# Five dummy products out, input blocks issued behind the first weight half, and the last weight sums moved behind group 0's weighing, in a two-layer decoder trunk

## The chip, the cores and the metric

The kernel runs on one core of one Trainium2 chip. The metric is the device time of one execution in microseconds; a time is the median of the runs shown.

## The reference

The reference computes two decoder layers over a residual stream h of 512 positions by 1024 features, all in float32. Only the first layer's start matters here:

```python
def dilated_mixer(xn, w_qkv, w_o, cos, sin):
    qkv = xn @ w_qkv                          # 12 heads of 64
    q, k, v = jnp.split(qkv, 3, axis=-1)
    ...                                       # rotary on q and k
    for g, (window, r) in enumerate(A_GROUPS):    # (128,1), (512,4), (2048,16): 4 heads each
        ...                                   # banded attention on every r-th position
        outs.append(o)
        lses.append(lse)
    alpha = jax.nn.softmax(jnp.stack(lses, axis=0), axis=0)
    o = jnp.concatenate([outs[g] * alpha[g][..., None].astype(outs[g].dtype)
                         for g in range(len(A_GROUPS))], axis=2)
    return o.reshape(B, T, A_WIDTH) @ w_o

def reference(...):
    h = x
    for l in range(DEPTH):                    # l = 0: dilated_mixer, l = 1: forgetting attention
        ...
        h = h + rms_norm(mix, g[1])
        f = conv_ffn(rms_norm(h, g[2]), w_up[l], conv_w[l], conv_b[l], w_down[l])
        h = h + rms_norm(f, g[3])
    return h
```

So three groups of heads are attended to separately, their outputs are weighed by a softmax over the groups ("weighing"), joined, and projected by w_o. Then follows a gated feed-forward network with a causal convolution of width 3.

## The kernel before

The 512 positions are four blocks of 128 on the partitions (`h[:, b, :]`). Every float32 product is made as three matmuls of a high part and a low part (high by high, high by low, low by high); the high part is a rounded copy made by ACT (ScalarE), the low part the rest, made by DVE (VectorE). TensorE (PE) sums them in eight PSUM banks of 128x512. All instructions of an engine run in the order in which the program wrote them; there is no scheduler that moves them. Waits between engines are by semaphores, which are put in from the tiles that each instruction reads and writes.

Nearly all loads go through one queue, SP's, in program order. Its semaphores are eight, taken in turn, so that an issue also waits for the landing of the one eight places before it. `Weights.load(n)` issues the loads up to weight piece n; `Weights.high` and `low` make the two parts of a piece, `get` hands out the next one and makes parts ahead (`W.ahead`).

**The start.** SP loads x in 256 KB pieces, block by block: `load_x(i, *blocks)` loads feature half i of these blocks. The first weight piece is loaded in two halves (`early[0][:, 0]`). `warm_up(n)` writes n dummy products of a zero tile into a bank that nobody reads; these come ahead of the first transposes. `gcol0` holds the norm gains of layer 0 as columns, which are multiplied into the weights. The lines:

```python
    W.load(1)
    load_x(0, 1, 2, 3)
    ...
    warm_up(4)
    ...                                    # transpose of the gain row, copy to gcol0
    warm_up(5)
    ...
    pool.tensor_copy(early[0][:, 1, 0:1], early[0][:, 0, 0:1])
    W.load(2)
    load_x(1, 0, 1)
```

The copy on POOL (GpSimd) reads the first weight half and writes one element a partition of the tile that the second piece is loaded into. So SP's load of the second piece stands until the first half has landed. After that block 0's first four feature chunks are transposed (`transposed0`, L1283), with two more dummies behind (`warm_up(2)`). ACT makes the high part (`high0`, L1287), DVE the low part (`low0`, L1291); `first_weight(k)` and `first_low(k)` (L1303, L1305, L1309) do so for the two halves of the first weight. `one0(b, kc, n)` is one of the three products of block b and feature chunk kc (L1320), and `split0(i, *blocks)` transposes and splits further blocks. Then q and k of group 0 follow for all blocks and chunks (`qk0`).

**The weight sums.** The down projection of the feed-forward networks is done with fewer products from sums of blocks of w_down. `down_sums` is a generator that makes these sums a step at a time: a step issues the loads of one pair of row blocks (L588 to L590), makes the four DVE sums (L593 to L596) of the pair one step before, and stores the pair one step before that to a buffer in device memory (`dT`, L601, two DMAs of 512 KB from SP). The generator `down0` has twelve pairs: (0,0) to (0,10) for layer 0 and (1,8) for layer 1, so 14 steps. Two steps are taken in `v_proj0`, and one behind each of the four weight pieces of three calls of `wide_proj` (q and k of group 1, q and k of group 2, v of groups 1 and 2). In the last of these the third step makes the sums of (1,8) and stores (0,10), and the fourth stores (1,8).

**From attention to the feed-forward network.** Behind the last `wide_proj`, written out by hand: `pv(g, pr)` multiplies probabilities and values (L1220, L1223), `weigh(g, pr)` transposes the group's factors on PE (L1239) and multiplies on DVE (L1241), `p_transpose` copies transposed probabilities on ACT (L1169), and `combine(g, pr)` makes the high and low part of the weighed output (L1251 on ACT, L1252 on DVE). Then SP loads the convolution's rows (L565, L566), two gain rows, two gains (L231), the last two pieces of w_o and the first of w_up (L50). The output projection (`Proj.finish`) does two of six chunks for blocks 0 and 1, then a hook transposes the convolution rows on PE (L573), copied by DVE (L575), then the two chunks for blocks 2 and 3, then the other four chunks. Before its first result is squared by ACT (L332), ACT makes the high parts of the next w_up pieces (L60) and DVE the low parts (L78), in program order. Of each block the projection's result is normed, added to h, normed again (`xn`, L311) and transposed (L361); the transposes of block 0 stand on PE between the projection's products.

Of the kernel before, what the change touches and what calls it, by code (L numbers as in the profile page):

```python
# [117 lines left out]
def trunk_kernel(ctx, tc, x, norm_gains, w_qkv_a, w_o_a, w_q_b, w_o_b, kv_norm, w_kvf, b_f,  # L118
                 w_up, conv_w, conv_b, w_down, rope, out):
    nc = tc.nc  # L120
    act, dve, pool, pe, sp = nc.scalar, nc.vector, nc.gpsimd, nc.tensor, nc.sync
# [8 lines left out]
    def t8(shape, dt=F32, name="t8"):  # L130
        return p8.tile(shape, dt, tag="t8", name=name)

    def t4(shape, dt=F32, name="t4"):
        return p4.tile(shape, dt, tag="t4", name=name)

    def t2(shape, dt=F32, name="t2"):
        return p2.tile(shape, dt, tag="t2", name=name)

    def bank(shape, name="bank"):
        return psp.tile(shape, F32, tag="ps", name=name)  # L140
# [16 lines left out]
    for g in range(3):  # L157
        for s in range(4):
            def f(raw, g=g, s=s):
                v = raw.rearrange("p (k t c) -> p k t c", k=2, t=2)  # L160
                src = wqkv.rearrange("(k p) (t c) -> p k t c", p=128, c=256)
                return [(v[:, k], src[:, 2 * s + k, g:g + 4:3, :]) for k in range(2)]
# [45 lines left out]
    early = []  # L208
# [13 lines left out]
    h = cst.tile([128, NB, D], F32, name="h")  # L222

    def load_x(i, *blocks):
        s = slice(i * 512, (i + 1) * 512)
        for b in blocks:
            sp.dma_start(h[:, b, s], xv[b * 128:(b + 1) * 128, s])
# [12 lines left out]
    zero = t2([128, 512], BF16, name="zero")  # L240
    dve.memset(zero, 0.0)
    warm = bank([128, 512], name="warm")

    def warm_up(n, c=512):
        for i in range(n):
            pe.matmul(warm[:, :c], zero[:, 0:128], zero[:, :c], start=True, stop=True)
    W.load(1)
    load_x(0, 1, 2, 3)
    rp = t4([128, 8, 32], name="rope")
    act.activation(sml.tile([128, 1], F32, tag="sd", name="warm"), eps_t, AF.Sqrt)  # L250

# [5 lines left out]
    pe.transpose(pg0, g_row, ident[:8, :8])  # L257
    gcol0 = sml.tile([128, 8], F32, tag="gcol0", name="gcol0", bufs=1)
    dve.tensor_copy(gcol0, pg0)
    warm_up(5)  # L260

    def columns(*ks):
        return [gcol0[:, k:k + 1] for k in ks]
# [14 lines left out]
    same = cst.tile([128, 4], F32, name="same")  # L278


    pool.tensor_copy(early[0][:, 1, 0:1], early[0][:, 0, 0:1])
    W.load(2)
    load_x(1, 0, 1)
    W.load(3)
# [4 lines left out]
    def mm3(o, ah, al, bh, bl, first, last, shared=False):  # L289
        pe.matmul(o, ah, bh, start=first, stop=False, skip_group_check=shared)  # L290
        pe.matmul(o, ah, bl, start=False, stop=False, skip_group_check=shared)  # L291
        pe.matmul(o, al, bh, start=False, stop=last, skip_group_check=shared)  # L292
# [285 lines left out]
    def down_sums(pairs, place, queue, lag, behind):  # L578


        live, n = [], len(pairs)
        for i in range(n + lag + behind):
            if i < n:
                l, j = pairs[i]
                a, b = place()
                live.append((a, b))
                r = w_down[l][j * 256:j * 256 + 256, :].rearrange("(c p) d -> c p d", p=128)
                sp.dma_start(a, r[0])  # L588
                sp.dma_start(b[:, 0:512], r[1, :, 512:1024])
                sp.dma_start(b[:, 512:1024], r[1, :, 0:512])  # L590
            if 0 <= i - lag < n:
                a, b = live[i - lag]
                dve.tensor_tensor(a[:, 0:512], a[:, 512:1024], a[:, 0:512], ALU.subtract)  # L593
                dve.tensor_tensor(a[:, 512:1024], b[:, 0:512], a[:, 512:1024], ALU.subtract)
                dve.tensor_tensor(b[:, 0:512], b[:, 0:512], a[:, 0:512], ALU.subtract)
                dve.tensor_tensor(b[:, 512:1024], b[:, 512:1024], b[:, 0:512], ALU.subtract)  # L596
            i -= lag + behind
            if i >= 0:
                l, j = pairs[i]
                for q, t in enumerate(live[i]):  # L600
                    queue.dma_start(dT[l][j, :, q * 1024:q * 1024 + 1024], t)  # L601
            yield
# [489 lines left out]
    def ax(g, b, kc):  # L1092
        return xs(xP if g else xT, kc, slice(b * 128, b * 128 + 128))
# [116 lines left out]
    def pv(g, pr):  # L1210
        o = bank([128, T], name="o_ps")
        for b in range(4):
            for hh in range(2):
                hd = 2 * pr + hh
                ov = o[64 * hh:64 * hh + 64, b * 128:(b + 1) * 128]
                vs = slice(hd * 64, hd * 64 + 64)
                if g == 0:
                    ks = [0, 1] if b else [1]
                    for k in ks:
                        pe.matmul(ov, V[g][:, b - 1 + k, vs], PT[g][hh][:, b, 2 * pr + k, :],  # L1220
                                  start=k == ks[0], stop=k == 1)
                else:
                    pe.matmul(ov, V[g][:, b, vs], PT[g][0][:, b, 2 * hh + pr, :], start=True, stop=True)  # L1223
        if g == 2:
            ow[g, pr] = o
            return
        ow[g, pr] = t = t2([128, T], name="ow")
        if g == 0:
            act.copy(t, o)
        else:  # L1230
            act.copy(t.rearrange("p (l r) -> p r l", r=4), o.rearrange("p (r l) -> p r l", r=4))
# [3 lines left out]
    def weigh(g, pr):  # L1235

        fb = bank([128, 4, 128], name="f_ps")
        for r in range(4):
            pe.transpose(fb[:, r, :], fac[g][:, r, 2 * pr:2 * pr + 2, :].rearrange("p h d -> p (h d)"), ident)  # L1239
        t = ow[g, pr].rearrange("p (l r) -> p r l", r=4)  # L1240
        dve.tensor_tensor(t, t, fb, ALU.mult)  # L1241

    def combine(g, pr):
        t = ow.pop((g, pr))
        if pr == 0:
            OT[g] = t8([128, 2, 2, T], F32R, name=f"OT{g}")
        hi, lo = (OT[g][:, part, pr, :] for part in range(2))
        if g == 2:
            t = t.rearrange("p (r l) -> p r l", r=4)
            hi, lo = (a.rearrange("p (l r) -> p r l", r=4) for a in (hi, lo))  # L1250
        act.copy(hi, t)  # L1251
        dve.tensor_tensor(lo, t, hi.bitcast(F32), ALU.subtract)  # L1252
# [27 lines left out]
    def transposed0(b, i):  # L1280
        pt = bank([128, 4, 128], name="xt_ps")
        for k in range(4):
            pe.transpose(pt[:, k, :], h[:, b, (4 * i + k) * 128:(4 * i + k + 1) * 128], ident)  # L1283
        return pt

    def high0(b, i, pt):
        act.copy(xT[0][i][:, :, b * 128:b * 128 + 128], pt)  # L1287

    def low0(b, i, pt):
        s = slice(b * 128, b * 128 + 128)  # L1290
        dve.tensor_tensor(xT[1][i][:, :, s], pt, xT[0][i][:, :, s].bitcast(F32), ALU.subtract)  # L1291

    def split0(i, *blocks):
        pts = [transposed0(b, i) for b in blocks]
        for b, pt in zip(blocks, pts):
            high0(b, i, pt)
            low0(b, i, pt)
# [9 lines left out]
    def first_low(k):  # L1307
        s, g = slice(512 * k, 512 * k + 512), columns(k)[0]
        dve.scalar_tensor_tensor(w0[:, 1, s], raw0[:, s], g, w0[:, 0, s].bitcast(F32), ALU.mult, ALU.subtract)  # L1309

    def weight0(s):
        if s not in ws:
            ws[s] = [t.rearrange("p (k c) -> p k c", k=2) for t in W.get()]
        return ws[s]

    def one0(b, kc, n):
        if b not in qk_banks:
            qk_banks[b] = bank([128, T], name="qk_ps")
        w, a = weight0(kc // 2), ax(0, b, kc)
        pe.matmul(qk_banks[b], a[n == 2], w[n == 1][:, kc % 2, :], start=kc + n == 0, stop=kc + n == KD + 1)  # L1320
# [13 lines left out]
    first_low(0)  # L1334
    first_weight(1)
    one0(0, 0, 0)
    warm_up(1, 128)
    one0(0, 0, 1)
    low0(0, 0, pt)
    one0(0, 1, 0)  # L1340
    first_low(1)
    one0(0, 0, 2)
    split0(0, 1)
    one0(0, 1, 1)
    one0(0, 1, 2)
# [42 lines left out]
    reorder(act.copy, 2, 3, parts=(0,))  # L1388
    sums = down_sums([(1, 6), (1, 7)], in_two, sp, 1, 3)
    next(sums)  # L1390
    def wide_proj(g, name, post, between):

        banks = [bank([128, T], name=name) for _ in range(4)]
        for s in range(4):
            w = W.get()
            wh, wl = (t.rearrange("p (k c) -> p k c", k=2) for t in w)
            for b in range(4):
                for k in range(2):
                    kc = 2 * s + k
                    ah, al = ax(g, b, kc)  # L1400
                    mm3(banks[b], ah, al, wh[:, k, :], wl[:, k, :], kc == 0, kc == KD - 1)
                if s == 3:
                    post(g, b, banks[b])
            for f in between[s]:
                f()
            next(down0, None)

    def v_post(g, b, o):
        if b == 0:
# [5 lines left out]
    down0 = down_sums([*[(0, j) for j in range(ND)], (1, 8)], in_one, sp, 1, 1)  # L1415
# [14 lines left out]
        [L(p_transpose, 1, 2), L(p_transpose, 1, 3), L(qk_transpose, 2, 0), L(qk_transpose, 2, 1)],  # L1430
        [L(qk_transpose, 2, 2), L(qk_transpose, 2, 3), L(scores, 2, 0, 1)],
        [L(scores, 2, 2, 3), factors],
        []])
    pv(0, 0)
    pv(0, 1)
    weigh(0, 0)
# [4 lines left out]
    pv(1, 0)  # L1441
    pv(1, 1)
    combine(0, 1)
    weigh(1, 0)
    weigh(1, 1)
    combine(1, 0)
# [420 lines left out]
```

## Time and profile before

| | us |
|---|---|
| runs | 1103.29, 1100.98, 1102.45 |
| median | 1102.45 |
| the profiled execution | 1101.57 |
| its span, from the first to the last instruction | 1099.8 |
| PE busy | 1092.0 (99%) |
| DVE busy | 877.4 (80%) |
| ACT busy | 671.1 (61%) |
| POOL busy | 174.4 (16%) |

The profile is of one execution. A row of the timeline reads: start in us from the span's start, duration in us, engine, source line, operation, what it writes from what it reads, shape, count; in brackets how long the engine stood idle before it and what ended that. PEld is PE's weight load, which overlaps PE. A "q" behind an engine is its sequencer: SPq rows are the issue of DMAs, not their transfer. Rows of equal operations are merged, and the duration is then that of all of them. A matmul's end is modelled, so that a stream of products is read by the distance of its starts.

### The profile page before, as it was taken

The page shows a single profiled execution, that of the slowest core. Times are in us where ns is not written, and L with a number is a line of the kernel's source. Part 1 is how long each engine was busy: PE and PEld are TensorE (multiplying, and loading weights), DVE is VectorE, ACT ScalarE, POOL GpSimd, SP SyncE. Part 2 cuts the span into 40 slices and gives each one's busy share as a digit, 9 for nine tenths or more (in the row PEclk, how much of TensorE's full clock was granted, in tenths as well). Part 3 has the DMA queues.
Part 4 walks back from the last instruction along what each step waited for, and adds up shares of the span by engine and source line. Part 5 has one row for each costly group of instructions (what it writes and reads, how often), then busy time and mean ns, then how long its engine had stood idle before and what let it go on. Part 6 is the DMA issues. An engine that isn't in the chain of part 4 may idle for free.

```text
span 1099.8 us, 18080 instructions
## 1 busy us (share of the span) xinstructions
PE 1092.0 (99%) x6600; PEld 951.0 (86%) x6600; DVE 877.4 (80%) x1496; ACT 671.1 (61%) x1116; POOL 174.4 (16%) x246
## 2 busy tenths in 40 slices
PE   9999999999999999999999999999999999999997
PEld 6988889899999988888878888889899999988886
DVE  4897888888778689897687667858888788679994
ACT  6755575755656747576452587755756666647572
POOL 3633001311111211000000212101311111211000
PEclk9999999999999999999999999999999999999999
DMA  9699764467987979894446767784468878989872
GB/s 319 198 343 409 304 200 134 102 176 190 211 194 184 249 252 331 291 324 117 134 154 223 266 192 199 243 246 135 91 179 190 211 185 188 240 267 320 308 249 77
DMA packets 192130, 242.67 MB, mean 221 GB/s; under 512 B 12848, under 2 KB 138792, under 8 KB 192040
## 3 DMA queue, kind: packets, MB, share of 16 engines
q1 hardware_dynamic: 176408, 189.33, 53.2%
q0 software_dynamic: 14944, 52.18, 20.6%
q8 instruction: 52, 0.85, 0.3%
q14 instruction: 38, 0.31, 0.1%
q10 hardware_dynamic: 688, 0.01, 0.0%
HBM read 172.37 MB, written 39.73 MB: 193 GB/s over the span
## 4 chain that ended last, share of the span: by engine, by line
PE 99%; DVE 1%; issue 0%; ACT 0%; DVEq 0%; ACTq 0%
PE up L291 13%; PE up L290 13%; PE up L292 13%; PE acc L290 9%; PE acc L292 9%; PE acc L291 9%; PE v_ps L290 2%; PE v_ps L292 2%; PE v_ps L291 2%; PE qk_ps L1320 2%; PE pT_ps L1708 2%; PE o_ps L1723 2%; PE s_ps L1674 2%; PE qk_ps L290 1%; PE first L292 1%; PE first L290 1%
## 5 line engine op out<-in xcount | busy, mean ns | idle before, releaser
L290 PE MATMUL acc<-w 128*128 128x512 f32 (+1 forms) x311 | 120.6, 388 | 0.3 <-DVE mix L339 0.3
L292 PE MATMUL acc<-w 128*128 128x512 f32 (+1 forms) x311 | 120.4, 387 | 0.0
L291 PE MATMUL acc<-w 128*128 128x512 f32 (+1 forms) x267 | 103.2, 387 | 0.0
L290 PE MATMUL up<-xsh,w 128*128 128x256 f32 x352 | 99.6, 283 | 0.0
L291 PE MATMUL up<-xsl,w 128*128 128x256 f32 x352 | 99.6, 283 | 0.0
L292 PE MATMUL up<-xsh,w 128*128 128x256 f32 x352 | 99.6, 283 | 0.0
L78 DVE TENSOR_TENSOR w<-wraw,w 128x1024 fp32r<-128x1024 f32 x62 | 82.3, 1342 | 21.2 <-ACT w L60 19.2
L627 ACT ACTIVATE bb<-up,conv 128x512 f32<-128x512 f32 x80 | 59.5, 775 | 58.8 <-DVE up L1014 48.0
L60 ACT CAST w<-wraw 128x1024 fp32r<-128x1024 f32 x81 | 83.6, 1050 | 19.0 <-DMA wraw<-in_w_up_dram 8.2
L291 PE MATMUL up<-xbl,w 128*128 128x512 f32 (+1 forms) x276 | 93.5, 339 | 0.0
L291 PE MATMUL up<-xcl,w 128*128 128x512 f32 (+1 forms) x276 | 93.5, 339 | 0.0
L290 PE MATMUL up<-xbh,w 128*128 128x512 f32 (+1 forms) x276 | 93.5, 339 | 0.0
L290 PE MATMUL up<-xch,w 128*128 128x512 f32 (+1 forms) x276 | 93.5, 339 | 0.0
L292 PE MATMUL up<-xbh,w 128*128 128x512 f32 (+1 forms) x276 | 93.4, 338 | 0.0
L292 PE MATMUL up<-xch,w 128*128 128x512 f32 (+1 forms) x276 | 93.4, 338 | 0.0
L290 PEld LDWEIGHTS acc<-w 128*128 128x128 f32 x311 | 58.4, 188 | 12.4 <-DVE mix L339 0.7
L292 PEld LDWEIGHTS acc<-w 128*128 128x128 f32 x311 | 58.4, 188 | 12.0
L290 PEld LDWEIGHTS up<-xsh,w 128*128 128x128 f32 x352 | 67.6, 192 | 0.0
L291 PEld LDWEIGHTS up<-xsl,w 128*128 128x128 f32 x352 | 67.6, 192 | 0.0
L292 PEld LDWEIGHTS up<-xsh,w 128*128 128x128 f32 x352 | 67.6, 192 | 0.0
L628 DVE SCALAR_TENSOR_TENSOR bb<-up,conv,bb 128x511 f32<-128x511 f32 x80 | 59.5, 744 | 6.4 <-ACT bb L627 6.2
L630 DVE SCALAR_TENSOR_TENSOR bb<-up,conv,bb 128x510 f32<-128x510 f32 x80 | 59.9, 749 | 2.8
(316 smaller groups left out, 3104.5 us busy)
## 6 DMA issues: line engine op xcount, KB each, us to landing
wraw<-in_w_up_dram SPq DMA_DIRECT2D x88, 512.0 KB
w<-wraw POOLq DMA_DIRECT2D x32, 512.0 KB, 6.5
dT<-dsums SPq DMA_DIRECT2D x28, 512.0 KB
w<-wsum POOLq DMA_DIRECT2D x24, 512.0 KB, 5.8
dsums<-in_w_down_dram SPq DMA_DIRECT2D x22, 512.0 KB
dsums<-in_w_down_dram SPq DMA_DIRECT2D x44, 256.0 KB
hD<-hc POOLq DMA_DIRECT2D x44, 256.0 KB, 7.1
dact<-hD SPq DMA_DIRECT2D x44, 256.0 KB
```

What stands on the lines that cost most here:

```text
L60: (copy or self.nc.scalar.copy)(pair[:, 0], raw)
L78: self.nc.vector.tensor_tensor(pair[:, 1], raw, pair[:, 0].bitcast(F32), ALU.subtract)
L290: pe.matmul(o, ah, bh, start=first, stop=False, skip_group_check=shared)
L291: pe.matmul(o, ah, bl, start=False, stop=False, skip_group_check=shared)
L292: pe.matmul(o, al, bh, start=False, stop=last, skip_group_check=shared)
L627: act.activation(bb[:, s, :], ps, AF.Identity, bias=cp[:, 3, ch:ch + 1], scale=cp[:, 2, ch:ch + 1])
L628: dve.scalar_tensor_tensor(bb[:, s, 1:], ps[:, :T - 1], cp[:, 1, ch:ch + 1], bb[:, s, 1:], ALU.mult, ALU.add)
L630: dve.scalar_tensor_tensor(bb[:, s, 2:], ps[:, :T - 2], cp[:, 0, ch:ch + 1], bb[:, s, 2:], ALU.mult, ALU.add)
L1320: pe.matmul(qk_banks[b], a[n == 2], w[n == 1][:, kc % 2, :], start=kc + n == 0, stop=kc + n == KD + 1)
L1674: pe.matmul(sc[j, i][hh][:, :nn], qT[j][own, qp, i * 128:(i + 1) * 128], k[own, kp, :nn], start=qp + kp == 0, stop=qp == 1)
L1708: pe.transpose(o[:, k0 + k, :], p[:, hh, k * 128:(k + 1) * 128], ident)
L1723: pe.matmul(o[64 * hh:64 * hh + 64, i * 128:(i + 1) * 128], Vt[hd // 8][:, k, (hd % 8) * 64:(hd % 8) * 64 + 64], pT[j, i, hh][:, k, :], st ...
```

## The change

- The five dummy products behind `gcol0`, and one dummy of 128 columns between the first two products, are taken out. The product one0(0, 0, 2) comes ahead of one0(0, 1, 0).
- `load_x` of feature half 0 for blocks 2 and 3 moves from ahead of the POOL copy to behind it, and the copy now writes into block 2 of h. The second weight piece no longer has a wait of its own and stands behind these two loads in SP's queue.
- The last two steps of `down0` move from the last `wide_proj` to behind `combine(0, 1)`, ahead of group 1's weighing. In SP's order the load of one w_o piece comes ahead of the two stores of pair (0,10).

```diff
-    def warm_up(n, c=512):
+    def warm_up(n):
         for i in range(n):
-            pe.matmul(warm[:, :c], zero[:, 0:128], zero[:, :c], start=True, stop=True)
+            pe.matmul(warm, zero[:, 0:128], zero, start=True, stop=True)
     W.load(1)
-    load_x(0, 1, 2, 3)
+    load_x(0, 1)
...
     dve.tensor_copy(gcol0, pg0)
-    warm_up(5)
...
-    pool.tensor_copy(early[0][:, 1, 0:1], early[0][:, 0, 0:1])
+    pool.tensor_copy(h[:, 2, 0:1], early[0][:, 0, 0:1])
+    load_x(0, 2, 3)
     W.load(2)
     load_x(1, 0, 1)
...
     one0(0, 0, 0)
-    warm_up(1, 128)
     one0(0, 0, 1)
     low0(0, 0, pt)
-    one0(0, 1, 0)
     first_low(1)
     one0(0, 0, 2)
+    one0(0, 1, 0)
     split0(0, 1)
...
-    def wide_proj(g, name, post, between):
+    def wide_proj(g, name, post, between, sums=4):
...
-            next(down0, None)
+            if s < sums:
+                next(down0, None)
...
         [L(scores, 2, 2, 3), factors],
-        []])
+        []], 2)
     pv(0, 0)
     pv(0, 1)
     weigh(0, 0)
     weigh(0, 1)
     for b in range(4):
         p_transpose(2, b)
     combine(0, 0)
     pv(1, 0)
     pv(1, 1)
     combine(0, 1)
+    for _ in range(2):
+        next(down0, None)
     weigh(1, 0)
     weigh(1, 1)
```

## The prediction

> **What bounds the kernel now.** I read the page first (span, busy shares, chain), then the timeline where the three edits lie: the first 11 us, and 132 to 167 us.
>
> ```profile
> span 1099.8 us, 18080 instructions
> PE 99%; DVE 1%; issue 0%; ACT 0%; DVEq 0%; ACTq 0%
> ```
>
> TensorE (PE) is the whole chain. What moves PE's first dense products earlier, or puts a pause into PE later, moves the end one for one; all other engines matter only through such pauses. The execution profiled took 1101.57 us (1.77 around its span), 0.88 below the median of the runs, 1102.45. I work out a difference and add it to that median. 0.2% is 2.2 us, about what a measurement of this kernel can tell from no change.
>
> **Edit 1, the dummy products.** The first stretch of the timeline:
>
> ```profile
> 0.74 0.39 SPq L227 DMA_DIRECT2D h<-in_x_dram  x1
> 1.19 0.94 SPq L50 DMA_DIRECT2D wearly<-in_w_qkv_a_dram  x2
> 1.22 1.89 PE L246 MATMUL warm<-zero 128*128 128x512 bf16 x4 [1.22 <-DVE zero L241]
> 2.16 1.42 SPq L227 DMA_DIRECT2D h<-in_x_dram  x3
> 3.24 2.74 PE L246 MATMUL warm<-zero 128*128 128x512 bf16 x6
> 4.34 0.19 POOL L281 COPY wearly<-wearly 128x1 f32<-128x1 f32 x1 [2.17 <-DMA wearly<-in_w_qkv_a_dram]
> 4.55 0.89 SPq L50 DMA_DIRECT2D wearly<-in_w_qkv_a_dram  x2
> 4.50 0.15 PEld L246 LDWEIGHTS <-zero 128*128 128x128 bf16 x1 [0.28 <-issue]
> 4.91 0.75 DVE L1309 SCALAR_TENSOR_TENSOR w<-wearly,gcol,w 128x512 fp32r<-128x512 f32 x1
> 4.93 0.15 PEld L246 LDWEIGHTS <-zero 128*128 128x128 bf16 x1 [0.28 <-issue]
> 5.78 0.90 PE L1283 MATMUL xt_ps<-ident,h 128*128 128x128 f32 x4
> 6.51 0.59 PE L246 MATMUL warm<-zero 128*128 128x512 bf16 x2
> 6.71 0.58 ACT L1287 CAST xah<-xt_ps 128x512 fp32r<-128x512 f32 x1 [3.86 <-PE xt_ps L1283]
> 7.35 0.50 PE L1320 MATMUL qk_ps<-w,xah 128*128 128x512 f32 x1 [0.24 <-ACT xah L1287]
> 9.45 1.04 PE L1283 MATMUL xt_ps<-ident,h 128*128 128x128 f32 x8
> ```
>
> Dummies come 0.43 us apart (4.50 to 4.93), so the six at 3.24 keep PE until 5.8, when block 0 of x is transposed. The 5 removed ones give 2.1 us. Is block 0 there by then? The first weight half, issued at 1.19, has landed by 4.34, within 3.15; x, issued at 0.74, by the same delay by 3.9. The remaining dummy ends at 3.67. I start the transposes at 3.8, 2.0 earlier. ACT's high part follows them by 0.93 (5.78 to 6.71): 4.73 to 5.31. The two dummies that stay now run at the slow pitch, 4.5 to 5.4, and hold the first product until 5.4. Then one0(0,0,0) and (0,0,1) at 0.43 each; (0,0,2) needs the low part, which DVE can start at 5.66 (L1309 ends) and end at 6.35; (0,1,0) at 6.75; block 1's transposes (0.6) from 7.0, two more products, and the 8 transposes of blocks 2 and 3 start at 8.0 to 8.1 instead of 9.45: 1.4 us gained. Taking out the 128-column dummy and reordering (0,0,2) ahead of (0,1,0) is in that sum. From then on PE is dense before and after.
>
> **Edit 2, the x halves.** The copy on POOL that waits for the first weight half now writes into block 2 of h, so SP's issue of blocks 2 and 3 stands behind it, at 4.55 and 5.0 instead of 2.6 and 3.1; the second weight half and all of SP's queue up to the rope table come two issues (0.9 us) later. By the delay of 3.15 block 2 lands at 7.7 and block 3 at 8.2, needed at 8.0 and 8.5: nothing. If each took the 4.2 us that the row below allows for the second weight half (issued 4.55; the rope issue, eight places later, waited for its landing until 8.76), they would cost 0.7. I take nothing; bounds 0 to 0.7. Weight half 2 is first used by ACT at 11.04, later than 9.7.
>
> ```profile
> 8.76 0.36 SPq L286 DMA_DIRECT2D rope<-in_rope_dram  x1
> 11.04 2.85 ACT L64 ACTIVATE w<-wearly,gcol 128x512 fp32r<-128x512 f32 x4
> ```
>
> **Edit 3, the last weight sums.** Two steps of the generator down0 move. The first is four DVE sums of the pair (1,8) and the two DMAs that store pair (0,10); the second is two DMAs that store pair (1,8). Around their place:
>
> ```profile
> 132.63 0.68 DVE L593 TENSOR_TENSOR dsums<-dsums 128x512 f32<-128x512 f32 x1
> 134.80 0.69 DVE L596 TENSOR_TENSOR dsums<-dsums 128x512 f32<-128x512 f32 x1
> 135.41 1.22 DVE L78 TENSOR_TENSOR w<-wraw,w 128x1024 fp32r<-128x1024 f32 x1
> 136.54 2.15 DVE L1241 TENSOR_TENSOR ow<-ow,f_ps 128x512 f32<-128x512 f32 x2
> 137.80 1.06 PE L1239 MATMUL f_ps<-ident,fac 128*128 128x128 f32 x8 [0.30 <-DVE ow L1241]
> 134.39 2.06 ACT L1169 COPY PT<-pT_ps 128x512 f32<-128x512 f32 x4 [0.93 <-PE pT_ps L1167]
> 137.69 0.62 ACT L1251 CAST OT<-ow 128x512 fp32r<-128x512 f32 x1 [1.24 <-DVE ow L1241]
> 140.73 0.69 DVE L1252 TENSOR_TENSOR OT<-ow,OT 128x512 fp32r<-128x512 f32 x1 [1.45 <-ACT OT L1251]
> 141.34 2.07 DVE L1241 TENSOR_TENSOR ow<-ow,f_ps 128x512 f32<-128x512 f32 x2
> ```
>
> Without the sums, group 0's weighing (136.54) comes 2.8 us earlier on DVE, and PE's 0.30 wait goes: 0.3 gained, and nothing else, since PE had no other wait there. ACT's cast, which waited for DVE, now follows its four copies at 136.45 instead of 137.69, 1.24 earlier; with the front's 1.4 everything up to combine(0,1) comes 2.6 earlier. Its low part (140.73) is at 138.1, and the sums start behind it at 138.7 and end 2.86 later at 141.55. Before they ended at 135.5: **6.1 us later**. That is covered on DVE (its weighing of group 1 starts at 141.4, as before at 141.34). It is not covered on SP, which stands in order:
>
> ```profile
> 134.07 1.77 SPq L601 DMA_DIRECT2D dT<-dsums  x2
> 135.94 1.44 SPq L565 DMA_DIRECT2D cv_rows<-in_conv_w_dram  x3
> 139.41 1.06 SPq L50 DMA_DIRECT2D wraw<-in_w_o_a_dram  x2
> 140.56 12.66 SPq L50 DMA_DIRECT2D wraw<-in_w_up_dram  x6
> 146.40 0.44 PE L573 MATMUL cv_ps<-ident,cv_rows 44*128 44x44 f32 x4
> 149.32 0.33 DVE L575 COPY conv<-cv_ps 128x176 f32<-128x176 f32 x1
> 155.04 1.05 ACT L60 CAST w<-wraw 128x1024 fp32r<-128x1024 f32 x1 [0.66 <-DMA wraw<-in_w_up_dram]
> 156.00 0.58 ACT L332 ACTIVATE junk<-acc 128x512 bf16<-128x512 f32 x1
> 158.90 1.28 ACT L334 ACT_TABLE_LOAD   x1
> 163.75 1.42 DVE L311 SCALAR_TENSOR_TENSOR xn<-h,rs,gain 128x512 f32<-128x512 f32 x2
> 166.16 1.03 PE L361 MATMUL xt_ps<-ident,xn 128*128 128x128 f32 x8
> ```
>
> The store of pair (1,8) waits on SP for the sums. Behind it wait the convolution rows, two gain rows, two gains, the last two w_o weights and the first w_up weights: all issued 6.1 later. Two of them reach PE.
>
> First the hook, where PE transposes the convolution rows: PE would be there at 146.40-1.7 = 144.7, but the rows, last issued at about 143.5, land between 143.5 and 146.6 (0 to 3.15 after); I take 145.4. Then the output projection of blocks 2 and 3 needs PSUM banks that DVE frees (the group 2 combine and the copy at 149.32), at their old times, because the sums took the place of the gain on DVE. PE stands at its old times by 149.8: the 1.7 us are given back.
>
> Second, the w_up weights. ACT's cast of the fourth ended its wait for the DMA at 155.04 and the first squares of the projection (156.00) stand behind it in ACT's order. ACT waited there, so the loads set it: 161.1, end 162.2. Squares follow until 163.4, and DVE's low part of that weight (1.2) until 163.4; the table load waits for the DVE step after it: 163.5 to 164.8. From its end (160.18) to the end of xn (163.75 + 1.42 = 165.17) it took 4.99: xn at 169.8 instead of 165.17. PE's last four transposes of block 0 take half of 1.03 after that: 170.3 instead of 167.19, **3.1 later**. I take 3.0, since PE's slack there can hide a part. No later place gives this back, as PE is 99% busy.
>
> Sum against this execution: -1.4 (front) -0.3 (weighing) +1.7 (hook) +3.0 (transposes wait) = +3.0: 1104.6, and 1105.4 on the median.
>
> **A rule against edit 1.** A row of the chain of waits gives PE's later pitch:
>
> ```profile
> 10.48 6.85 PE qk_ps L1320 x30
> ```
>
> That is 0.23 us a product, where the dummies at 4.50 and 4.93 were 0.43 apart; the two dummies at 6.51 took 0.59 together, so PE was fast by about 6.5, after 5.3 us of work since 1.22. In the changed kernel PE may pause at 3.7 for block 0. If the count started again at 3.8, PE would be slow until 9.1: 2.6 us at nearly half speed, 1.2 us. The Trainium skill, page "TensorE: Matmul & The Clock Gate", Part 1, says that the array runs at half clock until one window of about 3.4 us was busy, and Part 4 that transposes do not count as busy in the same way; an estimate from one window more is 1.7 us, half of it, and the sum would be +4.7 by it. The trace agrees with a slow start, and nothing in it shows whether transposes count.
>
> **Rivals.**
> - Clock late: the mechanism just told, +1.2 on the forecast: 1106.6. For it: the removed dummies are those that filled that stretch. Against: the two that stay, the transposes and slow products fill 3.8 to 6.5. Chance 0.14.
> - The hook alone: the gain is given back at the convolution rows and banks, but the w_up loads do not come 6.1 later (they had up to 1.9 us of slack before xn bites: first half at 164.46, PE at 166.16, and would need a faster queue). Sum 0: 1102.4. Chance 0.14.
> - The sums are hidden: DVE's 1.45 idle and the earlier casts take them, and the loads behind the store still land in time; then front and weighing stand, -1.7 to -2.4 (with all 2.1 of the dummies): 1100.7. It decides at a store delayed by less than 1.9 us; the rows give 6.1. It is also how it would be if SP's order were other than the built order says. Chance 0.17, about half of it beyond 2.2 us.
> - Forecast, own range +1.9 to +4.1 (1104.3 to 1106.6): chance 0.55.
>
> Range: to 1107.6 at the top (clock late with 0.7 for edit 2), to 1101.2 below, which leaves out most of the third rival and no more. Slower by over 2.2 us: 0.48 of the forecast and all of clock late, 0.62. Faster: 0.08. Within: 0.30.
>
> **What would show it.** Right: the first qk product near 5.4 instead of 7.35, the 8 transposes near 8.0; the four sums near 137 to 142; the two stores and the convolution rows about 6 us later on SP; ACT's w_up casts waiting for DMA until 161; a PE wait for xn before L361 near 167 to 170. Wrong: that L361 row within 1 us of 166.16, or the sums before 138; or 0.43 us products beyond 8.5 (clock).

## Result and the profile after

The changed kernel takes 1105.53 us (median of 6 runs, 1105.18 to 1107.13), the kernel before 1101.30 us on the same chip (6 runs, 1100.63 to 1103.29). The ratio is 1.0037, with a 95% interval of 1.0026 to 1.0047: 4.1 us slower, 2.9 to 5.2. The forecast had been 1105.4, 3.0 above the median of before that was then known, 1102.45. The profiled execution took 1105.20 us. Two executions of one kernel below (edits 1 and 2), 1347.9 and 2202.59 us, are left out of every ratio.

The page of the kernel after, its span and its chain:

```profile
span 1103.4 us, 18071 instructions
PE 92%; issue 2%; DMA 2%; DVE 1%; ACT 1%; POOL 0%; SPq 0%; DVEq 0%; POOLq 0%; ACTq 0%
```

The span is 3.6 us longer, and PE has fallen from 99% to 92% of the chain. That share is no measure of the loss: where PE waited, the chain goes back along the work that it waited for, for some 88 us in all, while the waits themselves are short. Those of PE by releaser (us in total, times, longest) that before did not have:

```profile
PE xt_ps L361 <- DVE xn L311: 1.3, 1, 1.3
PE acc L291 <- DVE w L78: 0.4, 1, 0.4
PE acc L290 <- DVE OT L1252: 0.3, 1, 0.3
PE xt_ps L1283 <- DMA h<-in_x_dram: 0.3, 1, 0.3
PE g_ps L1465 <- DMA g_rows<-in_norm_gains_dram: 0.2, 1, 0.2
PE pT_ps L1710 <- ACT prob L1688: 0.2, 1, 0.2
PE acc L290 <- DVE conv L575: 0.2, 1, 0.2
```

They add up to 2.9 us. The front (the first 11 us) of the timeline after, and last the row of before that stands against its last row:

```profile
3.64 1.06 PE L1283 MATMUL xt_ps<-ident,h 128*128 128x128 f32 x4
5.38 1.22 PE L1320 MATMUL qk_ps<-w,xah 128*128 128x512 f32 x2
8.22 0.60 PE L1283 MATMUL xt_ps<-ident,h 128*128 128x128 f32 x4
9.09 0.66 PE L1283 MATMUL xt_ps<-ident,h 128*128 128x128 f32 x4 [0.27 <-DMA h<-in_x_dram]
10.28 0.62 PE L1320 MATMUL qk_ps<-w,xah 128*128 128x512 f32 x2
```

```profile
11.02 0.62 PE L1320 MATMUL qk_ps<-w,xah 128*128 128x512 f32 x2
```

The first product is 1.97 us earlier, at 5.38. The transposes of block 2 are 1.23 earlier; ahead of block 3 PE stands, because that block of x has not landed; and from there the stream is 0.74 early (10.28 against 11.02). From here on I give the place of PE as such a difference: the start of a product in a trace less the start of the same product in the trace of before.

The middle of the timeline after, by engine:

```profile
136.70 1.09 PE L1239 MATMUL f_ps<-ident,fac 128*128 128x128 f32 x8
139.25 0.68 DVE L593 TENSOR_TENSOR dsums<-dsums 128x512 f32<-128x512 f32 x1
141.43 0.69 DVE L596 TENSOR_TENSOR dsums<-dsums 128x512 f32<-128x512 f32 x1
142.03 2.08 DVE L1241 TENSOR_TENSOR ow<-ow,f_ps 128x512 f32<-128x512 f32 x2
140.69 1.77 SPq L601 DMA_DIRECT2D dT<-dsums  x2
142.57 1.45 SPq L565 DMA_DIRECT2D cv_rows<-in_conv_w_dram  x3
147.05 11.84 SPq L50 DMA_DIRECT2D wraw<-in_w_up_dram  x6
145.28 0.87 PE L573 MATMUL cv_ps<-ident,cv_rows 44*128 44x44 f32 x4
146.90 0.50 PE L290 MATMUL acc<-w,OT 128*128 128x512 f32 x1 [0.32 <-DVE OT L1252]
150.43 0.50 PE L290 MATMUL acc<-w,OT 128*128 128x512 f32 x1 [0.18 <-DVE conv L575]
156.10 0.50 PE L291 MATMUL acc<-w,OT 128*128 128x512 f32 x1 [0.39 <-DVE w L78]
160.94 1.05 ACT L60 CAST w<-wraw 128x1024 fp32r<-128x1024 f32 x1 [0.75 <-DMA wraw<-in_w_up_dram]
163.39 1.28 ACT L334 ACT_TABLE_LOAD   x1 [0.24 <-DVE vr L336]
168.24 1.42 DVE L311 SCALAR_TENSOR_TENSOR xn<-h,rs,gain 128x512 f32<-128x512 f32 x2
169.05 1.32 PE L361 MATMUL xt_ps<-ident,xn 128*128 128x128 f32 x8 [1.30 <-DVE xn L311]
```

The row of before that stands against 146.90:

```profile
146.94 0.50 PE L290 MATMUL acc<-w,OT 128*128 128x512 f32 x1
```

Read it as one chain. The sums stand on DVE at 139.25, 6.6 after their old place. SP's store waits for them, and the convolution rows, w_o and w_up stand behind it: all 6.5 to 6.6 later than before. PE is 1.1 early at 136.70 (front and weighing), back at its old time at 146.90, 0.64 late at 150.43, 1.28 late at 156.10 and 1.4 behind that wait. ACT's last cast ahead of the squares waits for its load until 160.94 instead of 155.04, the squares, the table load and xn follow, and PE stands 1.30 us ahead of L361. Behind those transposes it is 3.2 late, and at the end 3.6; the rest comes near 690 us, where one more wait appears.

### The profile page after: what moved, and what is told of

It is laid out like the page before. It is cut to its first block, busy times and chain, and to the rows that moved or that the text cites. A ratio compares the mean times of both kernels' runs of the same rounds, so it can differ in the third digit from the quotient of the medians.

```text
span 1103.4 us, 18071 instructions
## 1 busy us (share of the span) xinstructions
PE 1093.1 (99%) x6594; PEld 950.6 (86%) x6594; DVE 877.7 (80%) x1496; ACT 670.6 (61%) x1116; POOL 174.2 (16%) x246
## 4 chain that ended last, share of the span: by engine, by line
PE 92%; issue 2%; DMA 2%; DVE 1%; ACT 1%; POOL 0%; SPq 0%; DVEq 0%; POOLq 0%; ACTq 0%
PE up L291 13%; PE up L290 13%; PE up L292 13%; PE acc L290 8%; PE acc L291 8%; PE acc L292 8%; PE v_ps L290 2%; PE v_ps L292 2%; PE v_ps L291 2%; PE qk_ps L1320 2%; PE qk_ps L290 1%; PE first L292 1%; PE first L290 1%; PE first L291 1%; PE qk_ps L292 1%
```

## The experiments

Every kernel was timed beside the kernel before. A difference in us is the ratio less 1, times the median of before (1101.4 to 1101.8). The first three take the change apart.

**Edit 1 alone** (dummies out, one0(0,0,2) ahead of one0(0,1,0)):

```diff
-    warm_up(5)
...
-    warm_up(1, 128)
```

> Edit 1 alone on the kernel before. Theory (front): the trace after shows the eight transposes of blocks 2 and 3 starting at 8.22 instead of 9.45, 1.23 us early, of which 0.4 was lost because block 3 of x had not landed. With the x halves issued where they were, that loss is gone: qk products 1.2 us early from 10.3 us on, and nothing on SP moves behind it, so the end moves with them: about 1.2 us below before. Rival (DMA pace): the w_up loads at 150 to 155 us keep their times, and the output projection or a later stage waits for them: under 0.4 us below before. Rival (clock): the slow products persist beyond 8.5 us: a gain of less than 0.8 at 10.3 us already.

Ratio 0.9998 (0.9990 to 1.0007): -0.2 us, -1.1 to +0.8. The profiled execution took 1100.21, the lowest of its 11 runs (up to 1102.88), and in it the front's gain is there: PE is 1.67 early at 20 us, with the transposes of blocks 2 and 3 dense,

```profile
5.36 0.73 ACT L1304 ACTIVATE w<-wearly,gcol 128x512 fp32r<-128x512 f32 x1
7.79 1.03 PE L1282 MATMUL xt_ps<-ident,h 128*128 128x128 f32 x8
```

and still 1.37 early at the end. So the theory holds for this execution and fails for the median. What the runs show of the reason, and what they leave open, stands further down.

**Edits 1 and 2:**

```diff
-    load_x(0, 1, 2, 3)
+    load_x(0, 1)
...
-    pool.tensor_copy(early[0][:, 1, 0:1], early[0][:, 0, 0:1])
+    pool.tensor_copy(h[:, 2, 0:1], early[0][:, 0, 0:1])
+    load_x(0, 2, 3)
```

> Edits 1 and 2 on the kernel before, the weight sums where they were. Theory: the front is that of the changed kernel, 0.74 us early at 11 us, a wait of PE of about 0.3 us for block 3 of x ahead of its transposes; edit 2 costs 0.4 to 0.5 against edit 1 alone; the end is about 0.7 us below before. Rival: the gain is given back at the convolution rows whatever SP does: 0, as before.

Ratio 1.0002 (0.9993 to 1.0011): +0.2 us, where 0.7 below was expected, and not to be told from edit 1 alone. The trace tells more. A row of its timeline, and one of PE's waits:

```profile
5.81 0.72 ACT L1305 ACTIVATE w<-wearly,gcol 128x512 fp32r<-128x512 f32 x1 [0.48 <-DMA wearly<-in_w_qkv_a_dram]
```

```profile
PE pT_ps L1707 <- ACT prob L1685: 1.1, 1, 1.1
```

ACT waits for the second half of the first weight piece, though fewer loads run beside it; PE is 1.00 early at 20 us, and loses all of it in one wait near 690 us (at the end +0.34). Over the traces in which PE did not wait for the weight half, PE's place at 20 us was -1.46, -1.54 and -1.67 with edit 1 alone (one each of three kernels, two of them told of below) and -0.75, -0.95 and -1.00 with edits 1 and 2 (likewise). Between the means lie 0.66 us. Not all of it is edit 2: PE's products run at half speed, 0.43 us apart, until 4.5, 5.8 and 6.9 us in the first three traces and until 6.6, 7.2 and 7.3 in the others. The two traces nearest in this (6.9 and 6.6) lie 0.46 apart, and in the changed kernel PE falls from 1.23 to 0.74 early at block 3: edit 2 costs about 0.5.

**Edit 3 alone:**

```diff
-        []])
+        []], 2)
...
     combine(0, 1)
+    for _ in range(2):
+        next(down0, None)
```

> Edit 3 alone on the kernel before. Theory (additive): the sums follow combine(0,1), which without the front comes 0.7 us later than in the changed kernel, so the stores, the convolution rows and the w_up loads come about 7.3 us later than before instead of 6.6, and the end about 4.3 to 5.0 us above before. Rival (slack): the loads are paced by the DMA and come no later than in the changed kernel, so the end is at 3.5 to 4.2 above. Rival (the front is the cause): 2.5 us or less above before.

Ratio 1.0037 (1.0025 to 1.0049): +4.1 us, 2.8 to 5.4, all of the change's loss. Its trace ends 4.4 late, as the additive theory says, 0.8 later than that of the changed kernel; the medians (1105.64 and 1105.53) do not show that difference, so they do not show the front's 0.7. That the front is the cause is ruled out.

**The stores on another queue.** The changed kernel, the stores of the last two pairs issued by POOL:

```diff
-                    queue.dma_start(dT[l][j, :, q * 1024:q * 1024 + 1024], t)
+                    (pool if n == ND + 1 and i >= ND - 1 else queue).dma_start(dT[l][j, :, q * 1024:q * 1024 + 1024], t)
```

> The changed kernel, but the DMAs that store the pairs (0,10) and (1,8) are issued by POOL instead of SP. DVE's four sums stay behind combine(0,1). Theory (SP's order is the price): the convolution rows are no longer behind the stores, they are issued before 136 us, ACT's w_up casts are not later than before, PE does not wait for xn ahead of L361 near 169 us; what stays is DVE's order, 0.6 us late at the first bank of block 3 (150.43 in the changed kernel): 0.3 to 1.1 us above before. Rival (DVE's time is the price: the low parts of w_up and the squares follow the sums on DVE): no change from the changed kernel, 4 us above before.

Ratio 1.0015 (1.0007 to 1.0024): +1.7 us, 0.8 to 2.6; more than half of the loss is gone with nothing on DVE moved. In its timeline and its waits of PE:

```profile
133.42 1.11 SPq L565 DMA_DIRECT2D cv_rows<-in_conv_w_dram  x3
141.82 2.05 DVE L1241 TENSOR_TENSOR ow<-ow,f_ps 128x512 f32<-128x512 f32 x2
166.65 1.03 PE L361 MATMUL xt_ps<-ident,xn 128*128 128x128 f32 x8
```

```profile
PE acc L290 <- DVE OT L1252: 1.0, 1, 1.0
PE pT_ps L1710 <- ACT prob L1688: 0.6, 1, 0.6
```

The convolution rows are issued 9 us earlier than in the changed kernel, and PE waits for no xn: L361 stands 0.5 late. That 0.5 is not all that DVE's order takes. PE comes to the transposes of the convolution rows 1.33 early and need not wait for the rows; but group 1's weighing still follows the sums, and PE waits 1.0 for its last low part. Its first product behind them is at 146.69, 0.25 early, and from the copy of L575 on it is 0.5 late. So both prices are real: DVE's order takes PE's lead and 0.5 more, 1.8 us, and SP's order about 2.5 (behind L361 PE is 2.7 later in the changed kernel, 0.2 of it from the front). Behind 600 us this trace loses 1.2 more, 0.8 of it at the wait near 690 us; that was not expected.

**The sums early.** Edit 1 without edit 2, and the two steps directly behind the weighing of group 0, where DVE waited for ACT's casts; stores on POOL, or on SP:

```diff
     weigh(0, 0)
     weigh(0, 1)
+    for _ in range(2):
+        next(down0, None)
     for b in range(4):
         p_transpose(2, b)
```

> Edit 1, the x halves where they were, the two steps of the sums moved only behind the weighing of group 0 (ahead of the copies of the transposed probabilities and of combine(0,0)), their four stores issued by POOL. From the traces: front -1.5 (edit 1 alone), weighing -0.3; DVE does the sums from about 134.4 to 137.3 us, in the time in which it waited for ACT's casts in the changed kernel (idle 1.04 and 1.70 us), and the weighing of group 1 starts at about 139 instead of 141.3; SP's loads lose the two stores ahead of them. Theory (SP's order was the price, and the place on DVE decides the rest): the hook and the projection stay 1.8 us early, the trace ends 1.5 to 1.9 us below before. Rival: the low part of combine(0,0), behind the sums, stops PE at the first projection products near 139: 0 to +1. In the median of many executions the trace's gain may be seen only in part, as with the dummies alone (trace 1.4 us, median 0.0).

> The same, but the four stores stay on SP. Theory (SP's order): the stores wait for the sums until about 137.4 instead of 134.1, so the convolution rows and the w_up loads come about 3.3 us later than before, ACT's fourth w_up cast at about 158 instead of 155, and PE, 1.8 us early, waits for xn ahead of L361: 1 to 2 us above before, that is 2.5 to 3.5 us above the same with POOL's stores. Rival (SP's order is not the price): the same time as with POOL's stores.

Ratio with POOL's stores 0.9994 (0.9985 to 1.0003), with SP's 1.0007 (0.9998 to 1.0016): -0.7 and +0.8 us, 1.4 apart in the order that SP's queue predicts, though less than the 2.5 to 3.5 expected, and with intervals that overlap a little. SP's version:

```profile
135.71 1.77 SPq L600 DMA_DIRECT2D dT<-dsums  x2
165.79 1.32 PE L360 MATMUL xt_ps<-ident,xn 128*128 128x128 f32 x8 [1.01 <-DVE xn L310]
```

PE, 1.9 early at the weighing, waits for xn here and is 0.1 early behind it. With POOL's stores that wait is absent, but PE comes there 2.5 us later in that trace; the last version below shows the same place without a wait and with PE early. The profiled execution with POOL's stores is its slowest of 11, 1102.96 (down to 1100.20), and shows what an execution of edit 1's front can lose:

```profile
7.18 0.72 ACT L1304 ACTIVATE w<-wearly,gcol 128x512 fp32r<-128x512 f32 x1 [1.86 <-DMA wearly<-in_w_qkv_a_dram]
7.96 0.50 PE L1319 MATMUL qk_ps<-w,xah 128*128 128x512 f32 x1 [1.30 <-ACT w L1304]
```

Here the second weight half landed at about 7.1, ACT scaled it then, and PE stood 1.30 us. Its windows (stretch, sum of PE, then PE, PEld, DVE, ACT, POOL busy, the granted clock, DMA share, GB/s) show what the pause did besides:

```profile
8.00:8.50 0.50, 0.50 (x3) 0.43 (x4) 0.50 (x1) 0.00 (x0) 0.00 (x0) 1.00 1.08 389
8.50:9.00 0.50, 0.50 (x5) 0.42 (x4) 0.19 (x1) 0.00 (x0) 0.00 (x0) 0.60 1.09 408
9.00:11.00 2.00, 2.00 (x9) 1.70 (x9) 0.69 (x1) 0.73 (x2) 0.00 (x0) 0.50 1.04 365
12.00:12.50 0.50, 0.50 (x4) 0.41 (x3) 0.34 (x2) 0.50 (x2) 0.00 (x0) 0.99 1.06 387
```

Half the clock from 8.6 to 12.0. PE is 1.40 late at 20 us, where edit 1's own trace had it 1.67 early: 3.07 between two executions of the same front. Less the 0.3 that this version gains at the weighing that is 2.8, and the times of the two executions differ by 2.75 (1102.96 and 1100.21). In the kernel before ACT does not come to this scaling before 7.2 (its row is 7.20, without a wait), so a landing at 7.1 would cost nothing there. This became the new theory: the dummies cover a landing that varies.

**Is the wait near 690 us the cause instead?** Layer 1's softmax on DVE waits there for an accumulating DMA. Its four pieces made by DVE:

```diff
-            W.minus()
-            W.low_added()
+            W.low()
```

> The kernel before, with one thing changed in layer 1's attention: the low parts of the four w pieces that POOL makes by an accumulating DMA (L98 in the last loop, after ACT's negative copy) are made by DVE in one step each. In the traces DVE's softmax step near 690 us waits until such a DMA has landed, 5.4 to 6.9 us after its issue, and PE loses 0 to 1.2 us there, another amount in each trace. Theory (that wait is where executions differ and where gains of the front go): the wait is gone, the time is that of before or up to 0.5 below, the runs lie closer together. Rival: DVE's four more steps of 1.2 us delay the softmax: 0.5 to 3 us above before.

> The same change with edit 1. Theory: the front's 1.4 us reach the end: 1.0 to 1.5 us below low_on_dve_before, in the median of the runs too. Rival: the gain is lost at another place or in the spread of the clock's start: no more than 0.4 below it.

Ratios 1.0010 (1.0001 to 1.0019) and 1.0003 (0.9995 to 1.0012): +1.1 and +0.3. The wait near 690 is gone in both traces, and a new one appears, at 837.5 us in the first and 835.9 in the second, behind which PE is 1.2 later in each:

```profile
PE up L290 <- DVE csum L970: 0.6, 1, 0.6
```

Both theories failed. Edit 1 is worth 0.8 by the two ratios (0.5 between the two medians), short of the 1.0 to 1.5 expected, with intervals that overlap. The wait near 690 costs PE 0 to 1.3 us in one trace or another, and in the trace of edits 1 and 2 it took the whole of the front's gain; that it does so in the median of edit 1 is not shown, nor ruled out.

**The landing itself.** The second weight half loaded behind all of x instead of ahead of blocks 1 to 3, with edit 1 and in the kernel before:

```diff
-    W.load(1)
-    load_x(0, 1, 2, 3)
+    raw = W.new_raw(0)
+    part = W.pieces[0](raw)
+    sp.dma_start(*part[0])
+    load_x(0, 1, 2, 3)
+    sp.dma_start(*part[1])
+    W.raw[0], W.n_dma = raw, 1
```

> Edit 1 alone, and the second half of the first weight piece is loaded behind all four blocks of x instead of ahead of blocks 1 to 3: issued at about 3.15 us instead of 1.66. Theory (the dummies covered a landing that varies): without them ACT makes the scaled second half as soon as it lands; in the traces with edit 1 that began at 5.2 to 5.8 us, but at 7.18 in one, where PE waited 1.3 us and then had half its clock from 8.6 to 12.0. With the load later it lands at 6.5 to 8 in every execution, PE waits 0.5 to 2 us, and in some executions the clock falls: 0.5 to 2.5 us above dummies_alone. Rival: the landing has nothing to do with the median: within 0.4 of dummies_alone.

> The same late load in the kernel before, whose dummies hold ACT's scaling until 7.2 us. Theory: most of the delay is covered: 0 to 0.6 us above before, at least 0.5 less than what the same load costs without the dummies. Rival (the load's place alone costs, whatever the dummies): the same loss as without them.

Ratios 1.0033 (1.0021 to 1.0046) and 1.0019 (1.0010 to 1.0028): +3.6 us without the five and a half dummies, +2.1 with them. Rows of the timeline, first without, then with dummies:

```profile
8.12 0.72 ACT L1308 ACTIVATE w<-wearly,gcol 128x512 fp32r<-128x512 f32 x1 [2.79 <-DMA wearly<-in_w_qkv_a_dram]
8.89 0.50 PE L1323 MATMUL qk_ps<-w,xah 128*128 128x512 f32 x1 [2.24 <-ACT w L1308]
```

```profile
9.29 0.50 PE L1324 MATMUL qk_ps<-w,xah 128*128 128x512 f32 x1 [1.78 <-ACT w L1309]
```

And the window from 10 to 12 us of each, in the same order (PE's busy time and count alone, then the granted clock, DMA share and GB/s):

```profile
10.00:12.00 2.00, 2.00 (x9) 0.50 1.05 362
```

```profile
10.00:12.00 2.00, 2.00 (x17) 1.00 1.05 364
```

The weight half landed at 8.1 and 8.5, later than the 6.5 to 8 I had allowed, so both sizes were short. But the same delayed load turns edit 1 from -0.2 into +3.6, 3.8 us, and costs 2.1 with the dummies: they cover 1.7 of it. A landing this late sets the front once the dummies are out, and its price is a wait plus, in the one, half the clock for one stretch.

**Asking for the second half later** in edit 1's front: block 1's products with the first half come ahead of one0(0,1,n):

```diff
-    first_weight(1)
     one0(0, 0, 0)
...
     low0(0, 0, pt)
+    pt = transposed0(1, 0)
+    high0(1, 0, pt)
+    first_weight(1)
     one0(0, 0, 2)
+    low0(1, 0, pt)
     first_low(1)
+    for n in range(3):
+        one0(1, 0, n)
...
```

> Edit 1, but what needs the second weight half comes later: block 1 of x is transposed behind one0(0,0,1), its cast stands on ACT ahead of the scaling of the second half, and block 1's three products with the first half come ahead of one0(0,1,n). So ACT scales from about 7.6 us and PE needs it at about 8.3, as late as before (7.9) though five and a half dummies are gone. Theory: the median shows what the good traces of edit 1 show: 0.8 to 1.4 us below before. Rival: the spread has another origin (the clock's start, or the landing waited for near 690 us): 0.4 below before or less.

Ratio 1.0009 (1.0000 to 1.0018): +1.0 us, where 0.8 to 1.4 below was expected. The trace shows what went wrong in one execution:

```profile
7.38 0.66 PE L1282 MATMUL xt_ps<-ident,h 128*128 128x128 f32 x4 [1.23 <-DMA h<-in_x_dram]
```

Now block 1 of x is asked for at 6.1, and it is not there before 7.4 in this execution; the clock falls again (8.6 to 12.0). So it is not that one load alone: the third load of the queue came at 7.1 in one trace, the fourth at 7.4 in another. The recorded rival, another origin of the spread, is not ruled out by this run.

**A version from these readings.** Two dummies out instead of five and a half, and the sums early with POOL's stores:

```diff
-    warm_up(5)
+    warm_up(3)
...
     weigh(0, 1)
+    for _ in range(2):
+        next(down0, None)
...
```

> The kernel before with two of its dummies out instead of five and a half (three stay behind gcol0, and the one of 128 columns, and the old order of one0), and the sums right behind the weighing of group 0 with their stores on POOL. Theory (the dummies cover landings that vary up to 7.2 us; the sums cost nothing where DVE waits anyway): two dummies are 0.85 us; where the second weight half has landed by 6.3 us the front keeps all of it, where it lands at 7.2 PE waits 0.5 us at most and its clock stays; the weighing gives 0.3: 0.6 to 1.2 us below before in the median. Rival (any shortening of the front is lost to the landings): 0.3 below before, no more. If the clock falls in the front of the trace, the theory is wrong in that execution.

Ratio 0.9988 (0.9979 to 0.9997): -1.3 us, -2.3 to -0.3, below the kernel before by an interval that only just leaves out no change, and so well below the changed one. Its 11 runs lie from 1099.42 to 1101.15.

```profile
6.48 0.72 ACT L1305 ACTIVATE w<-wearly,gcol 128x512 fp32r<-128x512 f32 x1
8.74 1.04 PE L1283 MATMUL xt_ps<-ident,h 128*128 128x128 f32 x8
135.09 0.68 DVE L593 TENSOR_TENSOR dsums<-dsums 128x512 f32<-128x512 f32 x1
165.05 1.03 PE L361 MATMUL xt_ps<-ident,xn 128*128 128x128 f32 x8
```

PE is 0.72 early at 20 us, 1.1 at the weighing, 1.1 ahead of L361 without a wait, 0.8 to 0.9 at the end: here the sums cost neither SP's price nor DVE's. The version makes two changes at once, and no run tells their shares apart.

## Why the prediction was right, and where not

- **The sign and the main step were right.** The store behind SP's queue was forecast 6.1 later (6.6), the fourth w_up cast at 161.1 (160.94), the table load at 163.5 (163.39), the end of xn at 169.8 (168.24 + 1.42 = 169.66), PE behind the first transposes 3.1 late (3.2). That SP's order, and not DVE's time, makes PE wait for xn is shown by the stores on POOL, with which this wait is gone.
- **The time of 1105.4 is in part luck.** The difference was forecast as 3.0 and measured as 4.1 (2.9 to 5.2; 3.6 in the trace), and the kernel before was 1.15 faster beside the changed one than when the forecast was made; the two nearly cancel.
- **The front was mis-sized:** -1.4 taken, -0.74 found. Edit 1 by itself gave -1.5 to -1.7 in its good executions. The step that failed is "I take nothing" for edit 2: block 3 landed at 9.0 instead of 8.2, and there PE fell from 1.23 to 0.74 early, 0.5 us, inside the prediction's own bounds of 0 to 0.7. The other 0.2 stood before that: the transposes of block 2 were at 8.22 instead of 8.0 to 8.1, as products were 0.43 apart until 7.3.
- **The weighing's 0.3 was right:** PE at 137.80 moves from 0.74 to 1.1 early and its wait is gone.
- **The hook:** PE was at its old time at 146.90, as forecast, and the 1.7 given back were 1.1, all that it then had. That it came to the rows at 145.28 (145.4 forecast) is a coincidence: the forecast waits there for the rows, but PE came as its own products ended, 0.6 less early than forecast. Behind that it waited 0.35 for the last rows and a gain row, ahead of a wait for DVE's low part that ended later. So DVE's order sets this step: with the stores on POOL the rows were early and the lead was lost all the same. Then a term is missing: "covered on DVE" failed by 0.7, since the front came 0.7 later than I took it, and the sums 0.55 (139.25, not 138.7); group 1's weighing began at 142.03 instead of 141.34, and PE was 0.64 late at 150.43. The wait for the w_o piece at 156.10 was not in the sum either. Neither changes the end: PE then has less slack ahead of xn, and xn's time sets it.
- **The wait for xn** is only 1.30 instead of about 3, because 1.4 had been lost before it. Over the stretch PE goes from its old time to 3.2 late, much as forecast (3.0).
- **The rivals.** The hook alone and the hidden sums are out by the wait at L361. The clock: full speed began at 7.3 in this trace instead of 6.4, which accounts for the 0.2 told above. (It is read from the products, 0.43 us apart before and 0.23 after, where the profile's clock record begins; ahead of it the granted clock reads 1.00 all the same.) But the mechanism, a count that starts again without the dummies, is not what the traces show: in four traces with all dummies the clock rose at 4.9, 6.4, 6.6 and 7.5, in nine with five and a half fewer at 4.5 to 7.3. The Trainium skill, page "TensorE: Matmul & The Clock Gate", Part 1, calls the window free-running and the rise different from run to run, by 0.5 us either way; the traces agree that it differs, but over 3 us.
- **Two figures of the prediction do not come out of its own terms.** The top of the range, 1107.6, would be 1105.4 + 1.2 + 0.7 = 1107.3, and the slack ahead of xn, 1.9, is 166.16 - 164.46 = 1.7 by its rows. The forecast does not rest on either.
- **What the prediction did not have** is that edit 1's gain is not in the median at all. It took one execution's landing times for the landing times.

What stays open is why the median of edit 1 shows nothing. The two profiled extremes speak for the landing, and so does, less strictly, the version with three dummies kept. Against it as the only cause: of seven traces with this load in its place and the dummies out, one has the late landing, too few for a median. And in two of the other six PE had the front's gain at 20 us and lost it further on: in that of edits 1 and 2 near 690 us, in that of the early sums with SP's stores at xn and then 1.5 us more, most of it near 690 and 884 us. No middle execution of edit 1 itself was profiled.

## What to carry to other kernels

Before a step with a store is moved, write down what stands behind that store on its queue; here eight small issues, two w_o pieces and the first weights of the next stage went out 6.6 us later for a move that saved PE 0.3, and another queue gave more than half of the loss back. Then write down what stands behind the moved step on its own engine: the sums took 1.8 us from PE by DVE's order behind combine(0, 1), and nothing where DVE had been waiting anyway. Filler work at the start may look like idle time made visible while it covers loads whose landing varies; it is safer to take out what the latest landing seen allows than what one trace allows. A single profile may be the best or the worst execution of its kernel, so read its time against the spread of the runs first.

## What was unexpected of the hardware

- A 256 KB load issued at 1.66 us, beside one to three other loads, was used by ACT at 5.2 to 5.8 us in six traces and at 7.2 in one, up to 2 us apart; three of the six have the same queue order as the one.
- A pause of PE of 1.23 to 2.24 us soon after the clock had risen halved the clock for one stretch of 3.4 us (8.6 to 12.0 twice, 9.4 to 12.8), in three traces; the one with 1.23 had a second pause, of 0.45 us, at 8.3. In all three the fall came 3.4 us after the rise (5.2, 5.1 and 6.0). A pause of 1.78 (7.5 to 9.3) in another trace did not halve it. The same page of the Trainium skill, "TensorE: Matmul & The Clock Gate" (Part 1), speaks of an idle window of about 3.4 us for the fall; these pauses were shorter than that, and the trace decides. In the trace without a fall the clock rose at 4.9, so that stretches of 3.4 us counted from there would cut the pause in two at 8.4; this fits, and was not tried by itself.
- The accumulating DMA that layer 1's softmax waits for near 690 us took 5.4 to 6.9 us from issue to release over five traces, and PE lost 0 to 1.3 us there.
